# Moving stores and the long convolution's sample part behind the next pair of weight loads in SyncE's queue

## The chip, the cores and the metric

The kernel runs on one core of a Trainium2 chip. A core has five engines with a queue of instructions each: TensorE (PE in the profile; its weight loads are shown as PEld), VectorE (DVE), ScalarE (ACT), GpSimd (POOL) and SyncE (SP). Each engine works its own queue off in order, and engines wait for each other with semaphores. In this kernel SyncE issues nearly all DMA transfers, loads and stores alike: an instruction of SyncE that waits for the data of a store keeps every load behind it in the queue.

The metric is the device time of one execution in microseconds; less is better.

## The reference

The reference is one step of a two-layer decoder trunk for 512 prompt positions and 8 sample rows, of which each brings its own state. A layer normalises its input, projects it with one matrix to seven parts of 1024 columns, sends these through an mLSTM branch and a convolution branch, and merges the branches. Cut to what matters here:

```python
h = rmsnorm(x, norm_w) * (1.0 + scale) + shift
xm, zm, ga, gb, zc, gm, gc = jnp.split(h @ w_in, 7, axis=-1)

xm_c, mbuf = causal_dwconv(xm, mbuf0, mconv_w, mconv_b)      # width 4
xm_c = jax.nn.silu(xm_c)
# q, k from xm_c, v from xm, per head; gates i, f from q, k, v
hm, C, n, m = mlstm_chunkwise(q, k, v, i_pre, logf, C0, n0, m0)
y_m = ((norm(hm) * gn_w + skip * xm_c) * jax.nn.silu(zm)) @ w_br_m

u = ga * jax.nn.sigmoid(gb)
u, cbuf = causal_dwconv(u, cbuf0, cconv_w, cconv_b)          # width 31
u = jax.nn.silu(layernorm(u, cln_w, cln_b)) * jax.nn.silu(zc)
y_c = u @ w_br_c

merged = jax.nn.sigmoid(gm) * y_m + jax.nn.sigmoid(gc) * y_c
x = x + gate * (merged @ w_out)
```

The outputs are y and, for each layer, the new states of prompt and samples: the matrices C (with the vector n as a further column), m, and the last rows of the inputs of both convolutions (mbuf, cbuf). These states are what the moved stores write.

## The kernel before

**Layout.** Channels lie on the 128 partitions. A tile of activations holds one block of 128 channels for T = 520 columns, the 512 prompt positions and then the 8 samples; a 1024-wide tensor has KT = 8 such blocks. Every large product is run with operands split in two parts of a faster number format, high and low, with three products hi·hi, hi·lo and lo·hi.

**Weights.** `split_w` (line 161) brings weights in: for each of n blocks of 128 output channels it loads 512 KB to a buffer `raw` (line 165, SyncE), casts it on ScalarE to `whi` (line 171), and takes the rest `wlo` on GpSimd in four pieces of 256 columns (line 174). There are two raw buffers (RAWB = 2) and three pairs of whi and wlo (WB = 3). A load waits until its raw buffer has been read by GpSimd, and a cast until TensorE has finished with the whi that it overwrites. `dense` (line 178) multiplies one such block with 8 blocks of activations for both halves of the 520 columns, 48 matmuls in all. Most calls of split_w fetch a pair of blocks.

**Order of a layer.** First `gab(0)` makes block 0 of u = ga * sigmoid(gb) with `dense_pair`, which interleaves the two products with the making of h. Then come the four steps of the xm stage: `do_xm(h)` (line 597) makes two blocks of xm and their short convolution, `do_v(h)` and `do_qk(h)` make v, q and k of one head. Their weights are traced in the order xm0 (a pair), xm1 (a pair), v0, qk0, xm2, v1, qk1, and so on; v and qk come from the tensor wqkv, all others from wst. `do_v(h)` reads xms, the split xm of do_xm(h). After the gates come blocks 1 and 2 of u, and then a loop over the four heads (line 951). In each head two of the 8 samples are handled by `sample(b)` (line 778): it loads that sample's matrix C to a tile cb (line 780, 1028 KB), multiplies it with q (pqc, line 789), and the result is added to qc on VectorE (line 794). `update` then renews cb (lines 802 and 804) and stores it to o_C_s (line 807). The tiles cb share three buffers (S8B = 3) with others. In each head one further block of u is also begun with `gab_b` (line 547), which fetches that block's pair of weights and multiplies the first of them; the second product, `gab_a` (line 562), called nxt, is run in the next head. After the heads come gab(7), the gate zm, the merge gates, the layer norm of u, zc and the output products.

**The pieces that the change touches.** At its end `gab_a` for block k stores the last 30 rows of u to o_conv_p (line 568), calls `conv31_sample(k)` and appends the tasks of the prompt's long convolution to a list that VectorE works off later. `conv31_sample(k)` (line 505) is the long convolution for the 8 samples: a load of the 30 former rows to us (line 507, 120 KB), a copy of the new row into it (line 508, VectorE), the store of the new state to o_conv_s (line 509), a multiplication with the taps on GpSimd (line 512), the sum over the taps (line 513) and the addition of the bias (line 514), both on VectorE. The tile us has one buffer, so the load for the next block waits for the store of the last. `do_xm` loads the three former rows of the short convolution to xw (line 623) and stores the new ones to o_mconv_s (line 625).

**What sets the order on an engine.** The program is traced in the order of the text, and then the builder makes each engine's queue: among the instructions whose inputs are there by its own timetable it takes the one that was traced first. So an engine's queue need not follow the text; the first matmuls of xm0, for instance, are run among those of gab(0). `tc.issue_after(i)` puts a tie on what is traced inside it: those of these instructions that are on i's engine come behind i in its queue. It is an order of issue alone, with no wait for i to be done.

Of the kernel before, what the change touches and what calls it, by code (L numbers as in the profile page):

```python
# [23 lines left out]
TP = 512  # L24
# [9 lines left out]
W4 = 4  # L34
W31 = 31
# [38 lines left out]
def build(nc, tc, ctx, ap):  # L74
# [71 lines left out]
    def t520(name):  # L146
        return tmp.tile([128, T], F32, tag="t520", bufs=T5B, name=name)

    def rsqrt(vv, shape, tag):
# [8 lines left out]
            v.scalar_tensor_tensor(out=y, in0=t, scalar=1.5, in1=y, op0=ALU.add, op1=ALU.mult)  # L158
        return y

    def split_w(src, n, w=1024, place=(None, None)):
        out = []
        for i in range(n):
            sl = wts.tile([128, w], F32, tag="raw", bufs=RAWB, name="raw")
            nc.sync.dma_start(sl, src[:, i * w:(i + 1) * w])
            if place[i]:
                hi, lo = (a[:, 0:w] for a in place[i])
            else:
                hi = wts.tile([128, w], F32R, tag="whi", bufs=WB, name="whi")
                lo = wts.tile([128, w], F32R, tag="wlo", bufs=WB, name="wlo")  # L170
            s.copy(hi, sl)  # L171
            for c in range(0, w, 256):
                cs = slice(c, c + 256)
                g.tensor_tensor(out=lo[:, cs], in0=sl[:, cs], in1=hi.bitcast(F32)[:, cs], op=ALU.subtract)  # L174
            out.append((hi, lo))
        return out

    def dense(w, xh, xl, nk, evac, halves=(0, 1)):
# [137 lines left out]
    def pcol(vec, o, k):  # L316
        return vec[:, o + k:o + k + 1]
# [94 lines left out]
    for l in range(L):  # L412
# [49 lines left out]
        u = None  # L462
# [42 lines left out]
        def conv31_sample(k):  # L505
            us = sml.tile([128, W31, TS], F32, tag="us", bufs=1, name="us")
            nc.sync.dma_start(us[:, 0:W31 - 1], ap["conv"][l, k])
            v.tensor_copy(us[:, W31 - 1], u[:, k, TP:T])
            nc.sync.dma_start(ap["o_conv_s"][l, k], us[:, 1:W31])
            pr = tmp.tile([128, W31, TS], F32, tag="t520", bufs=T5B, name="upr")  # L510
            cw = vec[:, O_CCW + k * W31:O_CCW + (k + 1) * W31]
            g.tensor_tensor(out=pr, in0=us, in1=cw.unsqueeze(2).to_broadcast([128, W31, TS]), op=ALU.mult)
            v.tensor_reduce(out=u[:, k, TP:T], in_=pr.rearrange("p w b -> p b w"), op=ALU.add, axis=AX.X)
            v.tensor_scalar(out=u[:, k, TP:T], in0=u[:, k, TP:T], scalar1=pcol(vec, O_CCB, k), scalar2=None,
                            op0=ALU.add)
# [30 lines left out]

        def gab_b(k, raw=False, w=None, behind=None):
            wb, wa = w or split_w(ap["wst"][l, PR_GAB + k], 2)
            sg = t520("sg")

            def evb(c, p):
                if raw or w:
                    s.copy(sg[:, c], p)
                    if w and c is HALF[1]:
                        s.activation(sg, sg, AF.Sigmoid)
                else:
                    s.activation(sg[:, c], p, AF.Sigmoid)

            def eva(c, p):
                v.tensor_tensor(out=u[:, k, c], in0=p, in1=sg[:, c], op=ALU.mult)  # L560

            def gab_a():
                if w:
                    dense_pair(wb, wa, hh, hl, evb, eva, ahead, hook)
                    mm = None
                else:
                    mm = dense(wa, hh, hl, KT, eva)
                nc.sync.dma_start(ap["o_conv_p"][l, :, k], u[:, k, TP - W31 + 1:TP])
                conv31_sample(k)
                filler.extend(conv31_tasks(k))  # L570
                return mm

            mm = None
            if not w:
                dense(wb, hh, hl, KT, evb, (0,))
                with tc.issue_after(behind.ins) if behind else nullcontext():
                    mm = dense(wb, hh, hl, KT, evb, (1,))
                if raw:
                    s.activation(sg, sg, AF.Sigmoid)
            return gab_a, mm  # L580

        def gab(k, raw=False, w=None):
# [14 lines left out]
        def do_xm(h, between):  # L597
            ws = split_w(ap["wst"][l, PR_XM + h], 2)
            xm = s8.tile([128, 2, T], F32, tag="s4", bufs=2, name="xm")
            xms = s8.tile([128, 2, 2, T], F32R, tag="s8", bufs=S8B, name="xms")  # L600
            acs = sml.tile([128, 2, TS], F32, tag="acs", bufs=2, name="acs")
            for j in range(2):
                k = 2 * h + j
                if j:
                    between()

                def ev(c, p):
                    s.copy(xm[:, j, c], p)
                    s.copy(xms[:, 0, j, c], p)

                dense(ws[j], hh, hl, KT, ev)
                v.tensor_tensor(out=xms[:, 1, j], in0=xm[:, j], in1=xms.bitcast(F32)[:, 0, j], op=ALU.subtract)
                g.tensor_copy(mtail[:, k, :], xm[:, j, TP - W4 + 1:TP])
                cw = O_MCW + k * W4
                ac = pm("ac")
                s.activation(ac, xm[:, j, 0:TP], AF.Copy, scale=vec[:, cw + 3:cw + 4])
                for sft in range(1, W4):
                    v.scalar_tensor_tensor(out=ac[:, sft:TP], in0=xm[:, j, 0:TP - sft],
                                           scalar=vec[:, cw + 3 - sft:cw + 4 - sft], in1=ac[:, sft:TP],
                                           op0=ALU.mult, op1=ALU.add)  # L620
                s.activation(xc[:, k, 0:TP], ac, AF.Silu, bias=pcol(vec, O_MCB, k))
            xw = sml.tile([128, 2, W4, TS], F32, tag="xw", bufs=2, name="xw")
            nc.sync.dma_start(xw[:, :, 0:W4 - 1], ap["mconv"][l, h])
            v.tensor_copy(xw[:, :, W4 - 1], xm[:, :, TP:T])
            nc.sync.dma_start(ap["o_mconv_s"][l, h], xw[:, :, 1:W4])
            xp = sml.tile([128, 2, W4, TS], F32, tag="xp", bufs=2, name="xp")
            cw = vec[:, O_MCW + 2 * h * W4:O_MCW + (2 * h + 2) * W4].rearrange("p (j w) -> p j w", j=2)
            v.tensor_tensor(out=xp, in0=xw, in1=cw.unsqueeze(3).to_broadcast([128, 2, W4, TS]), op=ALU.mult)
            v.tensor_reduce(out=acs, in_=xp.rearrange("p j w b -> p j b w"), op=ALU.add, axis=AX.X)
            for j in range(2):  # L630
                s.activation(xc[:, 2 * h + j, TP:T], acs[:, j], AF.Silu, bias=pcol(vec, O_MCB, 2 * h + j))
            return xms
# [49 lines left out]
        with tc.issue_after(mm.ins):  # L682
            for r in range(6):
                for n, c in enumerate(HALF):
                    for j in range(4):
                        t, k = srcs[r * 4 + j]
# [91 lines left out]
        def sample(b):  # L778
            cb = s8.tile([128, KT, V1], F32, tag="s8", bufs=S8B, name="cb")
# [5 lines left out]
            for j in range(2):  # L785
                for h in range(H):
                    k = 2 * h + j
# [8 lines left out]
            def update(hs):  # L796
# [7 lines left out]
                        v.scalar_tensor_tensor(out=cb[:, 2 * h + j, :], in0=vb[:, h, :], scalar=wsk[:, h, j, b:b + 1],  # L804
                                               in1=cb[:, 2 * h + j, :], op0=ALU.mult, op1=ALU.add)
                if H - 1 in hs:
                    nc.sync.dma_start(ap["o_C_s"][l, b], cb)

            return update

# [423 lines left out]
```

## Time and profile before

| | us |
|---|---|
| median of 3 runs | 1245.87 |
| lowest and highest run | 1245.64, 1247.6 |
| the profiled execution | 1245.75 |
| its span, first to last instruction | 1244.0 |
| ScalarE busy | 550.0 |
| GpSimd busy | 648.6 |
| VectorE busy | 850.7 |

The mean granted clock of TensorE is 0.992 of full speed. All DMA queues move 177.23 MB, 142 GB/s over the span.

How to read the lines further down: times are in us from the start of the span unless they are marked ns. L165 is line 165 of the kernel. A name such as raw<-wst says what an instruction writes and reads. PE is TensorE's matmuls; SPq is SyncE's queue, in which a DMA line stands at the time of its issue, not of its landing. "xN" counts instructions. In a timeline the bracket at the end of a line is the idle time of the engine just before it, and what ended that. In the chain of work that ended last, each line is a start, a duration and the work that the next line waited for.

### The profile page before, as it was taken

What the parts mean: (1) busy time and instruction counts of PE and PEld (TensorE: products, weight loads), DVE (VectorE), ACT (ScalarE), POOL (GpSimd) and SP (SyncE); (2) the same over time, 40 slices, a digit from 0 to 9 for tenths busy, and PEclk for the clock granted to TensorE, in tenths of its full rate; (3) what the DMA queues carried; (4) which work ended last, traced back from release to release, by engine and by line L of the source; (5) the groups of instructions that cost most, each with busy time, mean ns of one, the idle gap of its engine ahead of it and who ended that gap; (6) DMA issues with size and microseconds to landing.
All of it is one profiled execution on the core that took longest, in us unless ns stands there. A gap on an engine that the chain in (4) does not pass through costs nothing.

```text
span 1244.0 us, 26981 instructions
## 1 busy us (share of the span) xinstructions
PE 1207.4 (97%) x10856; PEld 1161.5 (93%) x10856; DVE 850.7 (68%) x1719; ACT 550.0 (44%) x991; POOL 648.6 (52%) x869
## 2 busy tenths in 40 slices
PE   6999999999999999999999999999999999999996
PEld 5999898899999999999988988988999999999995
DVE  6874467676998896654258635667789999937424
ACT  4676556543422223532236656556333222335242
POOL 2575444457544444565627553555665544536571
PEclk9999999999999999999999999999999999999998
DMA  9423447742364242243913234575332222224222
GB/s 362 148 89 94 146 149 256 266 173 95 104 219 153 91 148 86 78 170 130 366 67 96 87 109 175 195 263 213 125 103 94 94 88 100 86 85 137 104 86 69
DMA packets 59934, 177.23 MB, mean 142 GB/s; under 512 B 13408, under 2 KB 21664, under 8 KB 55712
## 3 DMA queue, kind: packets, MB, share of 16 engines
q1 hardware_dynamic: 56928, 167.08, 38.8%
q10 hardware_dynamic: 2880, 8.42, 1.8%
q8 instruction: 85, 1.39, 0.5%
q14 instruction: 41, 0.34, 0.1%
HBM read 149.77 MB, written 25.71 MB: 141 GB/s over the span
## 4 chain that ended last, share of the span: by engine, by line
PE 87%; DVE 4%; issue 3%; ACT 3%; DMA 2%; POOL 1%; SPq 0%; DVEq 0%; ACTq 0%; POOLq 0%
PE pd L186 72%; PE pds L889 3%; PE ppv L855 2%; PE pcf L855 2%; DMA wada<-w_ada 1%; PE ada L293 1%; PE ptok L850 1%; ACT whi L171 1%; PE pqc L789 1%; POOL wlo L174 1%; PE pg L688 1%; PE pd L246 1%; DMA raw<-wst 1%; PE pth L946 1%; PE pu L885 0%
## 5 line engine op out<-in xcount | busy, mean ns | idle before, releaser
L174 POOL TENSOR_TENSOR wlo<-raw,whi 128x256 fp32r<-128x256 f32 x680 | 523.8, 803 | 498.9 <-ACT whi L171 490.5
L186 PE MATMUL pd<-hh,whi 128*128 128x260 f32 x1728 | 494.9, 287 | 0.0
L186 PE MATMUL pd<-hl,whi 128*128 128x260 f32 x1728 | 492.2, 285 | 0.0
L186 PE MATMUL pd<-hh,wlo 128*128 128x260 f32 x1728 | 491.8, 285 | 0.0
L171 ACT CAST whi<-raw 128x1024 fp32r<-128x1024 f32 (+1 forms) x174 | 179.4, 1032 | 365.2 <-PE pd L186 329.7
L186 PEld LDWEIGHTS pd<-hh,whi 128*128 128x128 f32 x1728 | 326.8, 189 | 3.6 <-issue 1.8
L186 PEld LDWEIGHTS pd<-hh,wlo 128*128 128x128 f32 x1728 | 326.9, 189 | 1.8 <-issue 1.2
L186 PEld LDWEIGHTS pd<-hl,whi 128*128 128x128 f32 x1728 | 326.5, 189 | 1.8 <-issue 0.6
L535 DVE SCALAR_TENSOR_TENSOR cv<-u,vec,cv 128x509 f32<-128x509 f32 (+6 forms) x448 | 296.8, 729 | 0.0
L804 DVE SCALAR_TENSOR_TENSOR cb<-vb,wsk,cb 128x257 f32<-128x257 f32 x128 | 75.0, 651 | 1.1 <-ACT cb L802 0.4
L186 PE MATMUL pd<-hmh,whi 128*128 128x260 f32 x256 | 72.3, 282 | 0.0
L186 PE MATMUL pd<-hml,whi 128*128 128x260 f32 x256 | 72.3, 282 | 0.0
L186 PE MATMUL pd<-hmh,wlo 128*128 128x260 f32 x256 | 72.3, 282 | 0.0
L186 PE MATMUL pd<-zl,whi 128*128 128x260 f32 x256 | 71.6, 282 | 0.0
L186 PE MATMUL pd<-zh,wlo 128*128 128x260 f32 x256 | 71.6, 282 | 0.0
L186 PE MATMUL pd<-zh,whi 128*128 128x260 f32 x256 | 71.4, 282 | 0.0
L186 PE MATMUL pd<-mh,whi 128*128 128x260 f32 x224 | 63.1, 282 | 0.0
L186 PE MATMUL pd<-mh,wlo 128*128 128x260 f32 x224 | 63.1, 282 | 0.0
L186 PE MATMUL pd<-ml,whi 128*128 128x260 f32 x224 | 63.1, 282 | 0.0
L326 DVE SCALAR_TENSOR_TENSOR xr<-pd,mod,xo 128x260 f32<-128x260 f32 (+1 forms) x32 | 14.8, 482 | 60.7 <-PE pd L186 33.6
L186 PE MATMUL pd<-xcs,whi 128*128 128x260 f32 x256 | 48.5, 289 | 1.0
L186 PEld LDWEIGHTS pd<-hmh,wlo 128*128 128x128 f32 x256 | 48.2, 188 | 0.0
(304 smaller groups left out, 2236.7 us busy)
## 6 DMA issues: line engine op xcount, KB each, us to landing
raw<-wst SPq DMA_DIRECT2D x160, 512.0 KB, 3.7
wada<-w_ada SPq DMA_DIRECT2D x36, 512.0 KB, 9.1
cb<-C SPq DMA_DIRECT2D x16, 1028.0 KB, 7.8
o_C_s<-cb SPq DMA_DIRECT2D x16, 1028.0 KB, 5.7
vb<-vsc SPq DMA_DIRECT2D x16, 514.0 KB, 6.3
wada<-w_ada ACTq DMA_DIRECT2D x12, 512.0 KB, 8.0
raw<-wqkv SPq DMA_DIRECT2D x8, 512.0 KB, 3.6
x<-x SPq DMA_DIRECT2D x4, 520.0 KB
```

Source lines behind the costliest of these rows:

```text
L171: s.copy(hi, sl)
L174: g.tensor_tensor(out=lo[:, cs], in0=sl[:, cs], in1=hi.bitcast(F32)[:, cs], op=ALU.subtract)
L186: mm = te.matmul(p[:, 0:HT], a[:, ws], b[:, k, HALF[c]], start=(n == 0), stop=(n == 3 * nk - 1))
L246: mm = te.matmul(p[:, 0:HT], a[:, ws], b[:, k, HALF[c]], start=(k == 0 and i == 0), stop=(k == KT - 1 and i == 2))
L293: mm = te.matmul(acc[32 * j:32 * j + 32, 0:128], cT[:, k, :], raw[k // 2][:, k % 2, j * 128:(j + 1) * 128], start=(n == 0), stop=(n == KT ...
L326: v.scalar_tensor_tensor(out=x[:, m, c.start:c.start + n], in0=p[:, 0:n], scalar=mod[:, 16 + m, 0:1], in1=xo[:, c.start:c.start + n], op0= ...
L535: v.scalar_tensor_tensor(out=acc[a][:, sft:TP], in0=u[:, k, 0:TP - sft], scalar=wcol(sft), in1=acc[a][:, sft:TP], op0=ALU.mult, op1=ALU.add)
L688: te.matmul(pgs[n][32 * j:32 * j + 32, 0:HT], vec[:, o:o + 32], (q, kk, vv)[t][:, k, c], start=(r == 0), stop=(r == 5))
L789: te.matmul(p[32 * h:32 * h + 32, 0:V1], zq[:, o:o + 32], cb[:, k, :], start=(j == 0), stop=(j == 1))
L804: v.scalar_tensor_tensor(out=cb[:, 2 * h + j, :], in0=vb[:, h, :], scalar=wsk[:, h, j, b:b + 1], in1=cb[:, 2 * h + j, :], op0=ALU.mult, op ...
L855: te.matmul(p, a, b, start=(first and n == 0), stop=(last and n == 2))
L889: te.matmul(p[:, 0:n], kk[:, 2 * h + j, t0:t0 + 128], q[:, 2 * h + j, t0:TP], start=(j == 0), stop=(j == 1))
```

## The change

A list `held` is kept beside split_w. Four kinds of SyncE work are no longer traced where they stood but put into that list as small functions: the store o_conv_p together with the whole of conv31_sample(k) (in gab_a), the store o_conv_s inside conv31_sample, the store o_mconv_s in do_xm, and the store o_C_s in update. Each call of split_w traces its loads, casts and splits as before; then it empties the list and traces what was in it, with a tie that puts SyncE's part behind the last of the loads just traced. What is appended while the list is worked off (o_conv_s, by conv31_sample) stays there until the next call of split_w. The operations of conv31_sample on VectorE and GpSimd get no tie, but they are traced later too.

```diff
+    held = []
+
     def split_w(src, n, w=1024, place=(None, None)):
         out = []
         for i in range(n):
             sl = wts.tile([128, w], F32, tag="raw", bufs=RAWB, name="raw")
-            nc.sync.dma_start(sl, src[:, i * w:(i + 1) * w])
+            load = nc.sync.dma_start(sl, src[:, i * w:(i + 1) * w])
...
             out.append((hi, lo))
+        with tc.issue_after(load.ins):
+            todo = held[:]
+            held.clear()
+            for issue in todo:
+                issue()
         return out
...
             v.tensor_copy(us[:, W31 - 1], u[:, k, TP:T])
-            nc.sync.dma_start(ap["o_conv_s"][l, k], us[:, 1:W31])
+            held.append(lambda: nc.sync.dma_start(ap["o_conv_s"][l, k], us[:, 1:W31]))
...
-                nc.sync.dma_start(ap["o_conv_p"][l, :, k], u[:, k, TP - W31 + 1:TP])
-                conv31_sample(k)
+                held.append(lambda: nc.sync.dma_start(ap["o_conv_p"][l, :, k], u[:, k, TP - W31 + 1:TP]))
+                held.append(lambda: conv31_sample(k))
                 filler.extend(conv31_tasks(k))
...
             v.tensor_copy(xw[:, :, W4 - 1], xm[:, :, TP:T])
-            nc.sync.dma_start(ap["o_mconv_s"][l, h], xw[:, :, 1:W4])
+            held.append(lambda: nc.sync.dma_start(ap["o_mconv_s"][l, h], xw[:, :, 1:W4]))
...
                 if H - 1 in hs:
-                    nc.sync.dma_start(ap["o_C_s"][l, b], cb)
+                    held.append(lambda: nc.sync.dma_start(ap["o_C_s"][l, b], cb))
```

## The prediction

> **What bounds the kernel now.** I read first the page's head and its table of engines, then the busy time of each engine by stage, then SyncE's waits and its queue in order of time, and last the chain of work that ended last. The page's head and first table:
>
> ```profile
> span 1244.0 us, 26981 instructions
> PE 1207.4 (97%) x10856; PEld 1161.5 (93%) x10856; DVE 850.7 (68%) x1719; ACT 550.0 (44%) x991; POOL 648.6 (52%) x869
> ```
>
> TensorE is busy for 1207.4 of 1244.0 us. The change removes no matmul, so all that it can win lies in the 36.6 us in which TensorE is idle, and in a lower clock after such idle time. Busy time by stage (stretch, length, then busy us of PE, PEld, DVE, ACT, POOL, granted clock, DMA share, GB/s) shows how little of that lies where the moved stores are. The rows are the xm stage of layer 0, its mLSTM heads, and the xm stage of layer 1:
>
> ```profile
> 41.00:130.00 89.00, 87.22 (x743) 83.49 (x745) 57.06 (x94) 60.65 (x135) 58.20 (x83) 1.00 0.33 101
> 160.00:292.00 132.00, 131.21 (x1070) 119.53 (x1069) 91.56 (x239) 69.41 (x127) 72.10 (x98) 1.00 0.54 194
> 655.00:741.00 86.00, 81.75 (x669) 78.39 (x671) 58.39 (x94) 56.60 (x129) 53.35 (x76) 0.98 0.32 98
> ```
>
> TensorE idles 1.78 us, 0.79 us and 4.25 us there. SyncE's queue on the other hand does stand behind stores (engine and line, what it waited for, us in all, times, longest):
>
> ```profile
> SPq L807 <- DVE cb L804: 79.9, 8, 10.7
> SPq L568 <- DVE us L508: 42.3, 8, 26.9
> ```
>
> Some 80 us before the stores of the C state (L807) and 42 us before o_conv_p (L568). That weights queue up behind them does not yet mean that TensorE waits: the C stores all lie in the heads, where TensorE lost 0.79 us in 132. So the 79.9 us are hidden, and taking them away is worth nothing by itself. The longest wait, over 26 us, is at the start of layer 1. SyncE's queue there, in order of time:
>
> ```profile
> 623.83 6.02 SPq L165 DMA_DIRECT2D raw<-wst  x2
> 656.41 0.34 SPq L568 DMA_DIRECT2D o_conv_p<-u  x1
> 656.84 0.38 SPq L509 DMA_DIRECT2D o_conv_s<-us  x1
> 657.33 0.37 SPq L165 DMA_DIRECT2D raw<-wst  x1
> 658.13 0.34 SPq L165 DMA_DIRECT2D raw<-wqkv  x1
> ```
>
> The weights go in the order xm0 (two loads), xm1 (two), v0, qk0. v0 is the first load from wqkv, so 657.33 is the second load of xm1, and the two under 623.83 are the second of xm0 and the first of xm1. The second of xm1 stands behind o_conv_p(0) and o_conv_s(0). This is the one place where the chain of work passes through a load behind such stores:
>
> ```profile
> 652.50 4.83 POOL wlo L174 x7
> 657.33 3.89 DMA raw<-wst
> ...
> 662.44 2.84 POOL wlo L174 x4
> ...
> 665.29 3.62 DMA raw<-wqkv
> ...
> 669.01 1.04 ACT whi L171
> ```
>
> The load at 657.33 lands, is cast and split on POOL until 665.28, only then is its raw buffer free for qk0 (665.29). qk0 lands at 668.91 and is cast on ScalarE at 669.01. ScalarE works in order, and behind that cast stand the copies of xm for which TensorE waits:
>
> ```profile
> 670.66 0.80 PE L186 MATMUL pd<-xms,whi 128*128 128x260 f32 x2 [2.67 <-ACT xms L609]
> ```
>
> This gap of 2.67 us is the largest that a weight load causes, and the prize of the change. **The clock** adds to it. Busy time in short stretches behind this gap, and in and behind another one at 152 us:
>
> ```profile
> 672.00:674.00 2.00, 2.00 (x11) 2.00 (x11) 2.00 (x5) 1.58 (x4) 1.53 (x3) 0.50 0.00 0
> 676.00:678.00 2.00, 2.00 (x19) 2.00 (x18) 2.00 (x4) 0.73 (x3) 2.00 (x3) 1.00 0.10 39
> 152.10:154.40 2.30, 0.03 (x1) 0.03 (x1) 2.23 (x7) 0.81 (x3) 1.73 (x3) 1.00 0.46 114
> 156.00:158.00 2.00, 2.00 (x11) 2.00 (x10) 0.97 (x2) 1.98 (x4) 0.00 (x0) 0.50 0.93 373
> ```
>
> After either gap the granted clock is 0.50 for a while, with 11 matmuls in 2 us instead of 19. The xm stage of layer 1 has a mean of 0.98 over its 86 us, so 86 x 0.02 / 0.5 = 3.4 us at half clock, and these cost 3.4 x (1 - 11/19) = 1.4 us. The place is therefore worth at most 2.67 + 1.4 = 4.1 us, 0.33% of the time.
>
> **The change part by part.** Nothing is added or removed: the same stores, the same loads, the same sample part. Each moved piece gets one tie of order: SyncE may not issue it before the last load of the next split_w. There is no new semaphore and no wait for that load to land. What counts is whether the tie turns an order round that stands in the trace.
>
> *C stores and mconv stores (16 and 8).* Value: nothing. The odd store of head 0 is tied to the second load of pair 4:
>
> ```profile
> 156.63 0.36 SPq L165 DMA_DIRECT2D raw<-wst  x1
> ...
> 187.42 0.34 SPq L807 DMA_DIRECT2D o_C_s<-cb  x1
> ...
> 194.34 0.34 SPq L780 DMA_DIRECT2D cb<-C  x1
> ```
>
> Loads run about a head ahead: the load has gone out 30.8 us before the store, so the tie holds already and forbids nothing. It is the same with the even stores, and with o_mconv_s, which gets tied to the load of the next v or qk. What hides these stores today hides them afterwards.
>
> *o_conv_p(0).* It is tied to the second load of xm0, which goes out at 623.83, 32 us ahead of it. Nothing ties it behind the pair xm1. This is the step on which I rest most: at the place where TensorE really waits, the tie points to a pair that is already out, and the 26 us of standing stays.
>
> *o_conv_s(0).* It is put into the list while the list is worked off behind xm0, so it waits for the next call and is tied to the second load of xm1. Here an order is turned: 657.33 comes before 656.84. The load moves up by 657.33 - 656.84 = 0.49 us. v0 does not suffer from the store now in front of it, since it waits for POOL until 658.1, and the store takes 0.38 us. In layer 0 the same two rows change places:
>
> ```profile
> 45.45 0.38 SPq L509 DMA_DIRECT2D o_conv_s<-us  x1
> 46.00 0.34 SPq L165 DMA_DIRECT2D raw<-wst  x1
> ```
>
> That is 0.55 us, but TensorE has no large gap behind it (1.78 us idle in the whole stretch, spread over several waits), so I count 0; the other end is 0.55 us.
>
> *conv31_sample (load of us, three DVE operations, one POOL multiplication).* The loads of us(0) and us(1) go later. They are 120 KB without a reader for many us, so 0. The DVE operations are traced later and may change places on VectorE. Where they stand today:
>
> ```profile
> 199.18 0.62 DVE L513 TENSOR_REDUCE u<-upr 128x8 f32<-128x248 f32 x1
> 199.84 0.40 DVE L514 TENSOR_SCALAR u<-u,vec 128x8 f32<-128x8 f32 x1
> ```
>
> The two take 1.02 us, and the addition to qc for which TensorE waits comes after them:
>
> ```profile
> 202.40 0.39 PE L855 MATMUL ppv<-v1h,Ph 128*128 128x258 f32 x1 [0.34 <-DVE qc L794]
> ```
>
> If they move behind it, 0.34 us is won in this head, and no more than the stage's whole idle time of 0.79 us in all heads, 1.6 us in both layers if layer 1 is like layer 0. If they move in front of something TensorE needs sooner, up to 1.02 us a head is lost, 8.2 us in eight heads. I take 0, since they are run when their input is there and VectorE is free, and the tie changes neither.
>
> **The sum.** In layer 1 the second load of xm1 is 0.49 us earlier, and with it everything in the chain above, up to TensorE's start at 670.66. The gap becomes 2.67 - 0.49 = 2.18 us. TensorE is the bound from there to the end, so the rest moves up by 0.49 us. The profiled execution took 1245.75 us, 1.75 us more than its span; 1245.75 - 0.49 = **1245.3 us**. The three runs shown have a median of 1245.87 (1245.64 to 1247.6), so the profiled one is an ordinary one, and two of three lie within 0.2 us of it. About 0.2%, 2.5 us, is what can be told from no change.
>
> A word on the half clock, since a smaller gap might lose it. The Trainium skill, page "TensorE: Matmul & The Clock Gate", section "HAM oscillation — how this bites in real kernels", gives as the rule that TensorE should have no idle gaps over about 3.4 us. By that rule the gap of 2.67 us would cost no clock, and nor would one of 2.18. The rows above speak against it: 0.50 after gaps of 2.67 and of 2.30 us. The same page, Part 1, says that the activity is counted in windows of 3413 ns that run free of the kernel; by that, the place of the gap in a window decides, and the half clock may go at 2.18 us.
>
> **The rivals.** (1) *The load also gets ahead of o_conv_p(0).* The tie does not ask for it, but the order is made anew when the program is built. The first four of the seven POOL pieces from 652.50 free the buffer at 652.50 + 4/7 x 4.83 = 655.26, and 657.33 then becomes 655.3: 2.0 us, a gap of 0.7 us. That is under a third of the gaps that brought the half clock, so I let it go too: 1245.75 - 2.0 - 1.4 = 1242.3. For it: only 1.1 us separate 655.3 from 656.41. Against it: both layers have the store first, and its place among the loads of xm1 is not touched.
>
> (2) *The gap of 2.18 us no longer brings the half clock.* 1245.3 - 1.4 = 1243.9. Against it: 2.30 us did bring it. For it: where below 2.30 us the limit lies, the rows do not show.
>
> (3) *The three DVE operations get out of the way of qc.* 1245.3 - 1.6 = 1243.7.
>
> (4) *Slower: C buffers come free too late.* The odd C store of a head is now traced behind the next head's loads, and cb has three buffers; the load at 194.34 waits for a buffer that a store empties. Its reader in this and the next head, by the chain, and the usual times to landing (KB each, us):
>
> ```profile
> 198.91 1.04 PE pqc L789 x16
> ...
> 226.77 1.01 PE pqc L789 x16
> ```
>
> ```profile
> o_C_s<-cb SPq DMA_DIRECT2D x16, 1028.0 KB, 5.7
> cb<-C SPq DMA_DIRECT2D x16, 1028.0 KB, 7.8
> ```
>
> The store has to go out by 226.77 - 7.8 - 5.7 = 213.3, which is 25.9 us later than today's 187.42. A whole head, 226.77 - 198.91 = 27.9 us, would be 2.0 us too late: two such stores in a layer, four in all, 8 us, 1245.3 + 8 = 1253.3; with half the places, 1249.3. For it: the text order does move by most of a head. Against it: the store is ready at 187.42, and nothing holds it once its load is out, at 156.63.
>
> **How the numbers follow.** Forecast (one pair of rows changes places, 1245.3, own range 1244.2 to 1247.4, the scatter of the runs shown): 0.50. Rival 1: 0.16. Rival 2: 0.10. Rival 3: 0.08. Rival 4, with the loss on VectorE: 0.16. Below 1243.3 lies rival 1, and 2 or 3 where they come with each other or with layer 0's 0.55 us, 0.06 of their 0.18: faster 0.22. Above 1248.3 lies rival 4 with a little scatter: slower 0.17. Within 0.2%: 0.61. The range reaches to rival 1 below and towards the milder half of rival 4 above: 1242.0 to 1249.0.
>
> **What would show it.** Right: in layer 1 o_conv_p still stands over 25 us and is issued at about 656.4, the second load of xm1 follows at about 656.8, o_conv_s behind it, and the gap before pd<-xms is about 2.2 us with clock 0.50 after it; the C stores lie where they were. Wrong: that load goes out before o_conv_p (rival 1); clock 1.00 in 670 to 680 (rival 2); no wait of ppv for qc (rival 3); a wait of pqc for cb in heads 2 and 3 (rival 4). If an engine's order changes over whole stages, the working above does not apply.

## The result and the profile after

| | before | after |
|---|---|---|
| median, us (7 runs each) | 1245.64 | 1252.34 |
| lowest and highest run | 1244.36, 1247.6 | 1249.7, 1255.06 |
| profiled execution, its span | 1245.75, 1244.0 | 1253.11, 1251.4 |
| mean granted clock | 0.992 | 0.991 |

The ratio is 1.0055, with a 95% interval of 1.0041 to 1.0068: slower by 6.7 us, above the range of 1242.0 to 1249.0. The profiled span is 7.4 us longer. From the page of after, the head, the engines, and two of the groups of instructions (line, engine, what it does, count, then busy us and mean ns):

```profile
span 1251.4 us, 26954 instructions
PE 1208.2 (97%) x10856; PEld 1161.4 (93%) x10856; DVE 837.9 (67%) x1719; ACT 550.3 (44%) x991; POOL 664.3 (53%) x869
...
L176 POOL TENSOR_TENSOR wlo<-raw,whi 128x256 fp32r<-128x256 f32 x680 | 541.6, 828 | 484.4 <-ACT whi L173 469.4
...
L811 DVE SCALAR_TENSOR_TENSOR cb<-vb,wsk,cb 128x257 f32<-128x257 f32 x128 | 62.0, 554 | 1.6 <-ACT cb L809 1.4
```

The same two groups before:

```profile
L174 POOL TENSOR_TENSOR wlo<-raw,whi 128x256 fp32r<-128x256 f32 x680 | 523.8, 803 | 498.9 <-ACT whi L171 490.5
...
L804 DVE SCALAR_TENSOR_TENSOR cb<-vb,wsk,cb 128x257 f32<-128x257 f32 x128 | 75.0, 651 | 1.1 <-ACT cb L802 0.4
```

TensorE's busy time is the same to 0.8 us, so nearly all of the 7.4 us is new idle time: 43.2 us instead of 36.6. Two groups that the change doesn't name have changed: GpSimd's split of the weights (wlo) takes 18 us longer, and VectorE's updates of C take 13 us less. TensorE's two longest waits (what it waited for, us in all, times, longest) are:

```profile
PE rms L200 <- ACT sq L221: 7.8, 4, 5.7
PE pqc L796 <- DMA cb<-C: 6.3, 4, 2.2
```

The first is as before (7.7 us there). The second is new, since the same view of before has none for pqc, and it is nearly all of the new idle time. It is the symptom named in rival 4. One of the four places, in order of time on TensorE:

```profile
257.35 1.08 PE L796 MATMUL pqc<-cb,zq 128*32 128x257 f32 x16
260.08 1.08 PE L796 MATMUL pqc<-cb,zq 128*32 128x257 f32 x16 [1.65 <-DMA cb<-C]
```

The 32 pqc of a head come in two halves, one for each of its two samples (the even one and the odd one); the second half waits. In layer 1, where the prediction put its gain, SyncE's queue and TensorE's gap are now

```profile
660.21 0.34 SPq L575 DMA_DIRECT2D o_conv_p<-u  x1
660.65 0.37 SPq L167 DMA_DIRECT2D raw<-wst  x1
661.13 0.37 SPq L516 DMA_DIRECT2D o_conv_s<-us  x1
```

```profile
675.10 0.51 PE L193 MATMUL pd<-xms,whi 128*128 128x260 f32 x2 [2.69 <-ACT xms L616]
```

The order is the forecast one, the load stands ahead of o_conv_s. The gap did not shrink: 2.69 us instead of 2.67. The chain of work that ended last says why:

```profile
660.65 4.91 DMA raw<-wst
```

It took 4.91 us to land instead of 3.89, which more than eats up the 0.49 us won at its issue. A smaller loss lies in the xm stage of layer 0, where TensorE has a new gap, and one that was 0.17 us before is longer:

```profile
70.34 0.39 PE L193 MATMUL pd<-xcs,whi 128*128 128x260 f32 x1 [1.12 <-DVE xcs L650]
...
83.47 0.51 PE L193 MATMUL pd<-xms,whi 128*128 128x260 f32 x2 [0.80 <-ACT xms L616]
```

**What stands differently in a head.** VectorE and GpSimd in head 1 of layer 0, first before:

```profile
206.63 0.87 DVE L912 SCALAR_TENSOR_TENSOR kw<-ptok,wsl,kwh 128x256 fp32r<-128x256 f32 x2 [0.29 <-ACT kwh L911]
...
208.45 6.77 DVE L804 SCALAR_TENSOR_TENSOR cb<-vb,wsk,cb 128x257 f32<-128x257 f32 x12
```

```profile
210.01 3.73 POOL L174 TENSOR_TENSOR wlo<-raw,whi 128x256 fp32r<-128x256 f32 x4 [5.74 <-ACT whi L171]
```

and after, with the durations (min/median/max, ns) of the four wlo pieces in the last fence:

```profile
208.94 0.87 DVE L919 SCALAR_TENSOR_TENSOR kw<-ptok,wsl,kwh 128x256 fp32r<-128x256 f32 x2 [0.35 <-ACT kwh L918]
209.74 0.64 DVE L520 TENSOR_REDUCE u<-upr 128x8 f32<-128x248 f32 x1
210.30 0.47 DVE L919 SCALAR_TENSOR_TENSOR kw<-ptok,wsl,kwh 128x256 fp32r<-128x256 f32 x1
210.69 0.22 DVE L521 TENSOR_SCALAR u<-u,vec 128x8 f32<-128x8 f32 x1
210.82 0.47 DVE L919 SCALAR_TENSOR_TENSOR kw<-ptok,wsl,kwh 128x256 fp32r<-128x256 f32 x1
211.21 4.84 DVE L811 SCALAR_TENSOR_TENSOR cb<-vb,wsk,cb 128x257 f32<-128x257 f32 x12
```

```profile
L176 POOL TENSOR_TENSOR wlo<-raw,whi x4: 728/742/4384, 212.3 to 218.0; 128x256 fp32r<-128x256 f32 x4
```

The sample part's reduce and bias (L520, L521) now stand between the key pieces, ahead of the run of 12 C updates. (A key piece is one of the four instructions kw in VectorE's rows.) Counted from the first key piece the run starts at 211.21 - 208.94 = 2.27 us instead of 208.45 - 206.63 = 1.82, so 0.45 us later. In this head GpSimd's first wlo piece then takes 4.38 us: it ends 0.6 us after VectorE's run, and the next pieces take 0.73 to 0.74 us, so it stood until the run was all but over. I call this a shut-out below; it is there in six of the eight heads. Before, the two engines took turns over this stretch, and the run took 6.77 us and the pieces some 0.9 us each. So the run starts later but, in a head with a shut-out, ends sooner: 7.11 us from the first key piece, not 8.59. With the last wlo piece the raw buffer comes free, and SyncE's queue stands behind that with the load of the next weights. Before:

```profile
213.77 0.33 SPq L165 DMA_DIRECT2D raw<-wst  x1
...
215.25 0.34 SPq L807 DMA_DIRECT2D o_C_s<-cb  x1
215.64 0.42 SPq L782 DMA_DIRECT2D vb<-vsc  x1
216.15 0.81 SPq L780 DMA_DIRECT2D cb<-C  x1
```

After:

```profile
218.76 0.33 SPq L167 DMA_DIRECT2D raw<-wst  x1
...
219.66 0.38 SPq L789 DMA_DIRECT2D vb<-vsc  x1
220.10 0.44 SPq L814 DMA_DIRECT2D o_C_s<-cb  x1
220.63 0.39 SPq L787 DMA_DIRECT2D cb<-C  x1
```

Before, the odd C store (L807) goes out at 215.25, just as VectorE's run ends (208.45 + 6.77 = 215.22), and the C load follows. After, VectorE is done at 216.05, but the odd store and the C load stand behind the weight load until 218.76. Counted from the first key piece again, the C load goes out at 11.7 us instead of 9.5, and the second half of the next head's pqc needs it. This gave the theories that the runs below had to tell apart: **A**, the shut-out of GpSimd makes the loss; **B**, the tied C stores free their buffers late (rival 4); later **C**, the time of issue of the C load; and **D**, the bytes queued for transfer ahead of it.

### The profile page after: what moved, and what is told of

It is laid out like the page before. It is cut to its first block, busy times and chain, and to the rows that moved or that the text cites. A ratio compares the mean times of both kernels' runs of the same rounds, so it can differ in the third digit from the quotient of the medians.

```text
span 1251.4 us, 26954 instructions
## 1 busy us (share of the span) xinstructions
PE 1208.2 (97%) x10856; PEld 1161.4 (93%) x10856; DVE 837.9 (67%) x1719; ACT 550.3 (44%) x991; POOL 664.3 (53%) x869
## 4 chain that ended last, share of the span: by engine, by line
PE 81%; DVE 6%; DMA 4%; ACT 3%; issue 1%; POOL 1%; SPq 1%; DVEq 0%; ACTq 0%; POOLq 0%
PE pd L193 68%; DMA cb<-C 3%; PE ppv L862 2%; PE pcf L862 2%; PE pds L896 1%; ACT whi L173 1%; DVE cv L542 1%; PE ptok L857 1%; DVE ac L625 1%; POOL wlo L176 1%; PE pg L695 1%; PE pd L253 1%; PE pqc L796 1%; PE ada L300 1%; DMA raw<-wst 1%
## 5 line engine op out<-in xcount | busy, mean ns | idle before, releaser
L176 POOL TENSOR_TENSOR wlo<-raw,whi 128x256 fp32r<-128x256 f32 x680 | 541.6, 828 | 484.4 <-ACT whi L173 469.4
L193 PE MATMUL pd<-zl,whi 128*128 128x260 f32 x256 | 71.6, 282 | 0.0
L193 PE MATMUL pd<-zh,wlo 128*128 128x260 f32 x256 | 71.6, 282 | 0.0
L811 DVE SCALAR_TENSOR_TENSOR cb<-vb,wsk,cb 128x257 f32<-128x257 f32 x128 | 62.0, 554 | 1.6 <-ACT cb L809 1.4
```

What stands on the lines that cost most here:

```text
L193: mm = te.matmul(p[:, 0:HT], a[:, ws], b[:, k, HALF[c]], start=(n == 0), stop=(n == 3 * nk - 1))
```

## The experiments

Before and the run in question share a chip in each comparison; the median of before was 1247.22 us for e1 to e4, 1246.09 for e5 to e8, 1246.47 for e9 to e11 and 1246.32 for e12 to e14. "wlo" is the busy time of the split's group on the page, "pqc waits" what TensorE's waits give for pqc, with the number of places; both are from the one profiled execution, the ratio is from all.

| run | median us | ratio to before (95%) | wlo us | pqc waits, us |
|---|---|---|---|---|
| e1_sample_back | 1245.16 | 0.9991 (0.9978 to 1.0004) | 522.9 | none |
| e2_sample_only | 1254.24 | 1.0062 (1.0040 to 1.0084) | 543.1 | 8.5 in 6 |
| e3_heads_only | 1256.40 | 1.0076 (1.0048 to 1.0103) | 539.9 | 10.1 in 5 |
| e4_sum_late | 1247.50 | 1.0003 (0.9991 to 1.0015) | 522.3 | none |
| e5_repeat_quarter | 1248.40 | 1.0014 (1.0004 to 1.0024) | 522.6 | 1.9 in 3 |
| e6_repeat_full | 1248.38 | 1.0019 (1.0007 to 1.0032) | 522.4 | 5.6 in 5 |
| e7_repeat_half_us | 1257.28 | 1.0084 (1.0064 to 1.0105) | 522.0 | 8.8 in 6 |
| e8_load_first | 1241.94 | 0.9967 (0.9954 to 0.9979) | 523.7 | none |
| e9_queue_only | 1247.23 | 1.0002 (0.9988 to 1.0016) | 523.9 | none |
| e10_changed_plus_quarter | 1248.98 | 1.0023 (1.0011 to 1.0035) | 522.7 | 4.7 in 6 |
| e11_first_block_only | 1248.32 | 1.0012 (1.0002 to 1.0022) | 524.7 | 0.5 in 1 |
| e12_changed_C_before_vb | 1247.53 | 1.0008 (0.9998 to 1.0018) | 543.6 | none |
| e13_repeat_C_before_vb | 1246.75 | 1.0002 (0.9990 to 1.0014) | 521.8 | 1.2 in 2 |
| e14_load_first_C_before_vb | 1242.17 | 0.9962 (0.9948 to 0.9977) | 523.9 | none |

**Which part of the change costs.** e1 takes the tie off o_conv_p and the sample part and keeps it on all other stores; e2 is its mirror image, and ties these two alone. Of e1 the edit against the changed kernel:

```diff
-                held.append(lambda: nc.sync.dma_start(ap["o_conv_p"][l, :, k], u[:, k, TP - W31 + 1:TP]))
-                held.append(lambda: conv31_sample(k))
+                nc.sync.dma_start(ap["o_conv_p"][l, :, k], u[:, k, TP - W31 + 1:TP])
+                conv31_sample(k)
```

> The changed kernel with o_conv_p and the long conv's sample part issued at once, as before the change; the stores o_C_s, o_conv_s and o_mconv_s stay tied behind the next pair of weight loads. Theory A (the sample part's two VectorE operations move into the key stage, start the run of 12 C updates later against ScalarE's cast of the next weight, GpSimd is then shut out of its first wlo piece until the run is over, and the raw load and the C load behind it go out late): the loss goes away, 1245.0 to 1246.5 us, no wlo piece over 1.7 us, no wait of pqc for cb over 0.3 us. Theory B (a tied C store frees its buffer late, so that the next C load is late): the loss stays, 1250 to 1253 us, with the waits of pqc for cb still there.

> The kernel before with only o_conv_p and the sample part tied behind the next pair of loads; o_C_s, o_conv_s and o_mconv_s are issued at once. Theory A: the whole loss is there, 1251 to 1253.5 us, wlo pieces of 4.3 to 4.7 us in about 6 of 8 heads, and a wait of pqc for cb behind each that has a next head. Theory B: no loss, 1245 to 1247 us.

As theory A had it, and against B: with the C stores tied and the sample part not, there is no loss and no wait; with the sample part alone, all of it. In e1 all computing engines work in the order of before, in e2 in that of the changed kernel. The next two split the sample part's effect. e3 ties only blocks 2 and up:

```diff
+                late = held.append if k >= 2 else (lambda f: f())
+                late(lambda: nc.sync.dma_start(ap["o_conv_p"][l, :, k], u[:, k, TP - W31 + 1:TP]))
+                late(lambda: conv31_sample(k))
```

> As the run with the sample part alone tied, but only for blocks 2 and up, so the start of each layer (blocks 0 and 1) is as before the change. Theory A, if the loss has two places (2.3 us in layer 0's start from the re-made order there, some 4.4 us in the heads): 1245.6 + 4.4 = 1250 us (1249 to 1251), with the waits for xcs at 69 us and xms at 83 us gone. If the start's order is the cause of the heads' loss too: about 1246 us.

e4 keeps every tie and SyncE's order, and pins the reduce and the bias of blocks 2 to 5 (one block in each head) behind the last C update:

```diff
             with tc.issue_after(kw.ins):
-                updates[1](range(H))
+                end = updates[1](range(H))
+            with tc.issue_after(end.ins):
+                while totals:
+                    totals.pop()()
```

> The changed kernel, all ties kept and SyncE's order the same, but the sample part's reduce and bias on VectorE pinned behind the last C update for blocks 2 to 5, so that the run of 12 follows the key pieces directly as before the change. Theory A: the first wlo piece comes 1.5 to 1.6 us into the run again, no piece over 1.7 us, no wait of pqc for cb, and 1252.3 - 4.4 = 1247.9 us (1247 to 1249; the 2.3 us of layer 0's start stay). Theory B: no change from the changed kernel, 1251 to 1253 us.

The heads alone bring the loss (e3, more than the 4.4 us expected), and moving two short VectorE operations out of the way takes it back (e4). So the ties on SyncE's queue cost nothing that can be told here, and what the later tracing of the sample part did to VectorE's order does. In e4's trace the two stand behind the run of 12, which takes 6.78 us again.

**Is it the shut-out?** The next three move no store. They work out a part of the last key piece a second time (128 columns; all 256; 256 and 64), which delays the run of 12; for e7:

```diff
+                        if a and b:
+                            for c in (256, 64):
+                                last = v.scalar_tensor_tensor(out=kt[:, b, 0:c], in0=pb[:, 0:c], scalar=ws[:, i:i + 1],
+                                                              in1=kwh[:, i, 0:c].bitcast(F32), op0=ALU.mult,
+                                                              op1=ALU.subtract)
```

> The kernel before, no store moved and SyncE's order unchanged; in each head half of the last key piece is worked out a second time (128 of 256 columns, one more VectorE operation, some 0.25 us) between the key pieces and the run of 12 C updates, so that the run starts about a quarter of a microsecond later against ScalarE's cast. Theory A (only the place in the run at which GpSimd asks counts): GpSimd's first wlo piece is asked for at 1.3 us of the run instead of 1.5; shut out in some or none of the heads; for each shut-out head with a next head the second pqc waits 1 to 2.5 us for cb. Time: 0.25 x 8 = 2 us more at most for the operation itself if VectorE's run is on the path, plus the waits: 1245.6 to 1252. Theory B (only moved stores cost): 1245 to 1247.6 us and no shut-out.

> As the run before with the whole last key piece repeated (256 columns, 0.4 us): the run starts 0.4 us, one operation's step, later against the cast, and GpSimd asks at about 1.15 us of it. Theory A by the place in the run alone: as in the changed kernel (asks at 1.02 to 1.12 us, shut out in 6 of 8 heads), 1250 to 1253 us. Theory A by the place within one 0.395 us step (1.54 less 0.39 is the same place in the step as before): never shut out, 1245 to 1248 us. Theory B: as before, no shut-out.

> As the run before with a further 64 columns repeated (two more VectorE operations in each head, some 0.5 to 0.6 us): GpSimd asks at about 1.0 us of the run, as in the changed kernel, though no store is moved (SyncE's order differs in one place a head: a weight load ahead of one C_p store). Theory A: first wlo pieces of 4.3 to 4.7 us in most heads, waits of pqc for cb behind them, 1250 to 1254 us. Theory B: as before, 1245 to 1248 us.

The delay came out larger than these texts expected: counted from the first key piece the run starts at 2.21, 2.34 and 2.66 us, against 1.82 before and 2.27 in the changed kernel. (e7 also differs in SyncE's order: in four heads a weight load goes out ahead of the even sample's C load. e1 and e4 have the same in four heads, and no wait.) In none of the three was GpSimd shut out. The four wlo pieces of a head in e7 (min/median/max, ns), and TensorE's next pqc:

```profile
L174 POOL TENSOR_TENSOR wlo<-raw,whi x4: 769/918/923, 240.2 to 242.7; 128x256 fp32r<-128x256 f32 x4
```

```profile
256.84 1.07 PE L789 MATMUL pqc<-cb,zq 128*32 128x257 f32 x16
259.56 1.08 PE L789 MATMUL pqc<-cb,zq 128*32 128x257 f32 x16 [1.64 <-DMA cb<-C]
```

The waits for cb are there all the same, and the more the later the run: 1.9, 5.6 and 8.8 us. The time is 0.14%, 0.19% and 0.84% longer, of which the first two can't be told apart. So theory A as I had put it falls: the shut-out is not the condition for a loss. But it adds to it: e5 and e6 have the delay of the changed kernel within 0.1 us and no shut-out, and lose 0.14% and 0.19% where the changed kernel loses 0.55%, of which e11 below gives some 0.12% to the start of layer 0. Nor does the place in the run at which GpSimd asks decide whether it is shut out: it asked at 0.97 to 1.10 us in e6 and was let in each time, and at 1.02 to 1.12 us in the changed kernel and was kept out in six heads of eight. What decides it stays open. e10 adds the quarter of e5 to the changed kernel:

> The changed kernel with half of the last key piece worked out twice, so that the run of C updates starts a further 0.25 us later and GpSimd asks at about 0.75 us of it, where in the run of half a microsecond it was let in at every head. Theory A: no shut-out, so the loss of the changed kernel goes: 1246 to 1248 us. Theory C: no shut-out, yet the run ends later (6.8 us from its start instead of 4.8), so the C load is as late as before or later and the loss stays: 1251 to 1256 us.

Neither theory's time came out: the shut-outs are gone and the loss is less than half, 0.23%, not nothing. So in the changed kernel a good part of the loss does pass through the shut-out, and some is there without it. The run starts at about 2.66 us here, as in e7, which lost 0.84%: the delay alone does not give the loss, and why the two differ is open.

**What makes the C load late.** e9 leaves all computing engines alone. It puts three small stores behind the odd C store; the C load then goes out behind them, and vb behind the C load:

```diff
                 if H - 1 in hs:
-                    nc.sync.dma_start(ap["o_C_s"][l, b], cb)
+                    st_c = nc.sync.dma_start(ap["o_C_s"][l, b], cb)
+                    if b % 2:
+                        with tc.issue_after(st_c.ins):
+                            for n in range(3):
+                                extra = dr.tile([128, 8], F32, name="extra", tag=f"extra{n}", bufs=2)
+                                nc.sync.dma_start(extra, cb[:, n, 0:8])
```

> The kernel before with nothing changed on any computing engine: behind the odd C store of each head SyncE issues three small stores (128x8 of cb, into a scratch), and the vb load changes places with the C load behind it, so that the C load goes out some 0.75 us later. Theory C (the path from the end of the run of C updates through the odd C store and the C load behind it, landing some 11 us later, to the next head's second pqc has no slack, and whatever makes the C load later shows there): second pqc waits of 0.3 to 1.5 us for cb in most of the 6 places, 1248 to 1253 us. Theory A (the shut-out of GpSimd makes the loss): no shut-out here, as before within 1 us.

SyncE's queue in e9:

```profile
216.71 0.34 SPq L807 DMA_DIRECT2D o_C_s<-cb  x1
217.10 3.03 SPq L812 DMA_DIRECT2D extra<-cb  x3
220.17 0.46 SPq L780 DMA_DIRECT2D cb<-C  x1
220.67 0.45 SPq L782 DMA_DIRECT2D vb<-vsc  x1
```

The C load goes out 3.46 us behind the odd store, not 0.90 as before, and TensorE waits for nothing. Theory C falls too. What is different is that vb is no longer ahead of it. Its time to landing shows that, in head 1 of layer 1 (KB, then us from issue to landing; it goes out at 828.16 before and at 832.39 in e9). Before:

```profile
cb<-C SPq DMA_DIRECT2D x1, 1028.0 KB, 11.1
```

In e9:

```profile
cb<-C SPq DMA_DIRECT2D x1, 1028.0 KB, 6.4
```

From the odd store's issue (827.25 and 828.95) that is 12.0 us before and 9.8 in e9: issued 2.5 us later, the load landed 2.2 us sooner. Before, over a head's quiet part and from the odd store to the second pqc (the last two columns are the share of the 16 DMA engines and the GB/s):

```profile
205.00:215.00 10.00, 10.00 (x87) 10.00 (x86) 9.10 (x21) 6.16 (x12) 3.73 (x4) 1.00 0.40 120
216.00:227.50 11.50, 11.50 (x85) 9.38 (x83) 4.86 (x14) 6.16 (x11) 6.18 (x8) 1.00 1.03 392
```

The DMA engines are full from the moment the odd store goes out, at the end of VectorE's run, until pqc. So I took it that a C load lands when what is queued ahead of it has been moved, and that it has next to no slack: the load above lands at 839.3, and the 32 pqc that need it for their second half start at 838.73 and take 1.95 us. The Trainium skill, page "DMA: Bandwidth & Descriptors", section "Two DMAs through the same engine are not ordered", says that within one queue of one DMA engine descriptors start in order and are pipelined; the trace agrees, since the load that was issued 2.5 us later landed no later once 0.5 MB ahead of it were gone. e12 and e13 put it to the test. Both only issue vb behind the C load, in the changed kernel and in that of e7:

```diff
-            nc.sync.dma_start(cb, ap["C0"][l, b])
+            load = nc.sync.dma_start(cb, ap["C0"][l, b])
...
+            with tc.issue_after(load.ins):
+                nc.sync.dma_start(vb.rearrange("p h c -> p (h c)"),
+                                  vsc[b].rearrange("h c -> (h c)").partition_broadcast(128))
```

> The changed kernel with one tie more: the load of vb (0.5 MB) is issued behind the C load of the same step, not ahead of it; all computing engines keep their order, and so the shut-outs of GpSimd. Theory D (what makes cb late is what is queued to be transferred ahead of it from the odd C store on: 1.05 MB of store, 0.53 MB of vb and, where the weight load was late, 0.65 MB more, against a date that leaves no slack): without vb ahead some 2.4 us come free, the waits of pqc for cb of 1.1 to 2.2 us go, and 1246 to 1249 us, the start of layer 0 still late. Theory A or C (the shut-out itself, or the C load's time of issue, makes the loss): 1251 to 1254 us, waits as in the changed kernel.

> The kernel before with some 0.55 us of key pieces repeated in each head, as in the run that lost 0.8%, and the load of vb behind the C load. Theory D: no wait of pqc for cb over 0.5 us, and within 2.5 us of before (1246 to 1249 us). Any theory in which the 0.55 us of VectorE work itself is on the path: 1250 to 1258 us as without the tie.

Theory D holds in both by the time, 0.08% and 0.02%. In e13 the waits go down from 8.8 us to 1.2 in two places, one of them 1.0 us and so over the half that was expected at most: with the run as late as that, vb isn't the whole of it. e12 still has shut-outs, in seven heads of eight, and the weight load still goes out late, yet the two halves of pqc follow each other without a wait, here and in every head:

```profile
L176 POOL TENSOR_TENSOR wlo<-raw,whi x4: 728/736/4393, 240.7 to 246.4; 128x256 fp32r<-128x256 f32 x4
```

```profile
247.17 0.33 SPq L167 DMA_DIRECT2D raw<-wst  x1
...
248.08 0.97 SPq L815 DMA_DIRECT2D o_C_s<-cb  x1
249.14 0.38 SPq L787 DMA_DIRECT2D cb<-C  x1
249.58 0.94 SPq L790 DMA_DIRECT2D vb<-vsc  x1
```

```profile
257.29 1.95 PE L797 MATMUL pqc<-cb,zq 128*32 128x257 f32 x32
```

**The start of layer 0.** e11 ties block 0 alone (`k == 0` in place of `k >= 2` of e3).

> The kernel before with only block 0 of each layer tied (o_conv_p and the sample part, behind the next pair), heads as before. If the start of layer 0 loses 2.3 us by its re-made order, as in the changed kernel: 2 to 2.5 us above before with waits for xcs near 69 us and xms near 83 us. If that loss was a matter of that one execution: within 1 us of before.

In between: 0.12%, 1.5 us with 0.2 to 2.7 as its interval. The wait for xcs came back, that for xms near 83 us did not (0.17 us, as before):

```profile
70.80 0.39 PE L193 MATMUL pd<-xcs,whi 128*128 128x260 f32 x1 [1.22 <-DVE xcs L651]
```

That is a second, smaller term. e12's 0.08% is of that size, but e4 has the wait too (1.1 us) and loses 0.03%, so its size is uncertain. The wait did not show in e2, whose computing engines have the same order as the changed kernel's, so it depends on small differences at the start that I haven't followed.

**What the change was after.** e8 is the kernel before with only block 0 of layer 1 put off, by two pairs and not by one, so that the second load of xm1 is free of o_conv_p:

```diff
+                if l and k == 0:
+                    held.append((1, lambda: nc.sync.dma_start(ap["o_conv_p"][l, :, k], u[:, k, TP - W31 + 1:TP])))
+                    held.append((1, lambda: conv31_sample(k)))
...
+            for n, issue in todo:
+                if n:
+                    held.append((n - 1, issue))
+                else:
+                    issue()
```

> The kernel before with only block 0 of layer 1 changed: its o_conv_p and the sample part are issued behind the second pair of loads (xm1's) instead of ahead of it; every other store is as before. If the wait of 2.67 us for xms in that stage, and the half clock behind it (1.4 us), come from the weight load that stands behind o_conv_p in SyncE's queue: the load goes out about 6 us earlier, the wait goes, and the time is 1242.3 us (1241.5 to 1243.9), 2 to 3.4 us under the kernel before of the same chip. If the wait has another cause (ScalarE or VectorE late with xms for its own reasons): within 1 us of before.

SyncE's queue, TensorE's gap, and the clock in the eight microseconds behind it (0.79 behind the gap of before and of the changed kernel, 670.6 to 678.6 and 675.1 to 683.1):

```profile
654.10 0.33 SPq L167 DMA_DIRECT2D raw<-wst  x1
655.16 0.34 SPq L579 DMA_DIRECT2D o_conv_p<-u  x1
```

```profile
667.97 0.51 PE L196 MATMUL pd<-xms,whi 128*128 128x260 f32 x2 [1.23 <-ACT xms L623]
```

```profile
668.00:676.00 8.00, 8.00 (x66) 8.00 (x67) 8.00 (x15) 5.90 (x14) 6.94 (x10) 1.00 0.26 84
```

0.33% faster, 4.1 us with 2.6 to 5.7 as its interval, better than both kernels. The way there was not quite the expected one: the load went out 3.2 us earlier, not 6, and 1.23 us of the gap stayed. The place itself gave 2.67 - 1.23 = 1.44 us of the gap and the 1.4 us of the half clock, some 2.9 us. The profiled execution, the fastest of the six, also has no half clock behind the gap at 154 us, which the edit doesn't touch (1.00 from 154.7 to 162.0 us, 0.78 from 154.4 to 162.0 before). So it is shown that more than half of the gap came from the load's place in the queue; that the medians give just the 4.1 us of the prediction's bound is luck. With e14 the vb load goes behind the C load as well:

> The version that puts layer 1's weight load ahead of block 0's stores (0.9967 of before), and the load of vb behind the C load. Theory D: the heads had no wait for cb in most executions, so only small ones go (0.0 to 0.1 us a head): 0.9955 to 0.997 of before, that is 1240.5 to 1243 us. If vb is late for the C updates: slower than 0.9967, 1243 us or more.

0.9962 against 0.9967: no difference that can be told. Before, the heads had no wait for cb, so there was nothing to win there.

## Why the prediction was wrong

- **The loss that weight loads cause lies at layer 1's xm stage, and is worth at most 4.1 us with the clock.** Right as to the place: e8, which really turns that order round, is faster. Of the size its trace shows 2.9 us. The half clock was taken as a fixed price of the gap, and it isn't one: in e7 and e1 the same place had gaps of 2.73 and 2.51 us and no half clock behind them (1.00 over the next 8 us).
- **The tie on o_conv_p(0) does not get the load ahead of it.** Right: the order after is the one forecast, and the long stand is still there (26.9 us at the longest).
- **o_conv_s(0) and the load change places, 0.49 us.** The order came, the gain did not. Mis-sized is the time to land: I took 3.89 us as fixed, and it was 4.91. Why it landed later I haven't settled. This made the forecast 0.5 us too low, not 7.
- **The start of layer 0: counted as 0, at best 0.55 us won.** It lost, some 1.5 us by e11 (0.2 to 2.7). The later tracing changed the order of VectorE, ScalarE and GpSimd there, which the prediction did not look at.
- **C and mconv stores: nothing.** Right, by e1. Rival 4 named the symptom, pqc waiting for cb, and a time of 1253.3 near the measured one, but its cause was the held C stores, and they cost nothing. That its time came near is luck.
- **conv31_sample's VectorE operations: "I take 0, since they are run when their input is there and VectorE is free, and the tie changes neither".** This is the step that failed. The operations are not run when VectorE is free: VectorE works in the order in which the program was built, and tracing them later changed that order. They came to stand among the key pieces, where they put off the start of the run of C updates by 0.45 us. In six heads of eight GpSimd was then shut out of its split of the weights until that run was over, the weight load waited for the split, and the odd store, vb and the C load went out behind the weight load, 2.2 us late in the head shown. TensorE then waited for that C load, 6.3 us in four places. With the two operations out of the way (e4) the loss is gone. The bound that I gave, up to 8.2 us, lies over the 6.7 us measured only by luck: it was the length of the operations times eight heads, and the loss came by another way, through what is queued behind them. Behind them stood a stretch of 11.5 us in which the DMA engines are full, up to the pqc that need the C load. I had read the heads as having slack, since TensorE lost only 0.79 us there in 132; but that row shows that a wait isn't there, and not how near it is. The prediction's last sentence names the case of an engine's order that changes over whole stages, but gives it no chance and no price.

## What to carry to other kernels

A function that is put off to move a store also moves whatever else it traces, and with it the order on other engines: compare the order of every engine, not only of the queue that was meant, and put off the bare store rather than the function around it (for o_conv_p no run here did that; the C stores, put off bare, cost nothing). A stage without waits may have next to no slack: look at whether the DMA engines are full up to the very moment at which a load is needed. And where several loads go out together, let the one that is needed first go first; here its place among the bytes counted for more than the time of its issue.

## What the runs showed of the hardware

VectorE and GpSimd have two ways of getting along in the same stretch. In the kernel before they took turns, 0.92 us a wlo piece and 0.88 us a step of VectorE while both ran; in six heads of the changed kernel GpSimd's first piece stood until VectorE's run was all but over, 4.35 to 4.69 us, and VectorE went on at its 0.40 us a step. The Trainium skill, page "SBUF — State Buffer", section "SBUF: two separate sides", says that the two engines share a pair of ports under an exclusive lock, held for a whole instruction by the one that starts first, while the other blocks fully. The turns of one instruction each agree with that. In the shut-out GpSimd was kept out over some nine further instructions of VectorE in a row; why in some heads it gets its turn after the next instruction and in others not until the run ends, though it asked within 0.1 us of the same place, the page does not say and no run here explains.

The length of a gap on TensorE did not by itself tell whether half clock follows. In layer 1's xm stage gaps of 2.67 us (before) and 2.69 us (changed) were followed by it, and one of 2.73 us (e7) was not: the clock was 1.00 from 675.3 to 683.3 us. In e12 a gap of only 1.45 us was followed by a clock of 0.53 from 71.6 to 75.2 us.
